# A two-layer decoder with a routed MoE on one core: scatter order, place of the overflow branch, token split and gather order changed

## The chip, the cores and the metric

The kernel runs on one core of one Trainium2 chip. The metric is the device time of one execution in microseconds (us). Engines are named as in the profile: PE is TensorE, DVE is VectorE, ACT is ScalarE, POOL is GpSimd, SP is the queue that issues the weight transfers.

## What is computed

Two layers over 256 tokens of width 1024, in float32. Each layer has a token mixer (a convolution and a pooling branch with gates) and a mixture of experts; the change lies in the second. The reference, cut to that:

```python
h2 = modulate(rms_norm(x, ffn_norm_g[l]), sh2, sc2)
x = x + g2[:, None, :] * hierarchical_moe(h2, ...)
# hierarchical_moe(t): 4 groups of 8 experts
group_probs = softmax(t @ w_rg + b_rg)
p_group, g_idx = top_k(group_probs, 1)
exp_logits = (t @ w_re + b_re).reshape(n_tok, 4, 8)
in_group = take_along_axis(exp_logits, g_idx[:, :, None], axis=1)[:, 0]
p_exp, e_idx = top_k(softmax(in_group), 2)
weights = p_group * p_exp / sum(p_exp)
out = sum over experts e of weight(t, e) * (silu(t @ w_g[e]) * (t @ w_u[e])) @ w_d[e]
```

Each token goes to two of 32 experts; an expert has a hidden width of 256, so its three matrices are 1 MB each.

## The kernel before, in words

**Weights.** All 298 MB of traffic are nearly the weights. SP issues them in a fixed order (`plan`, `issue`) into a ring of 14 slots of 1 MB and some spare tiles; a slot is filled again when PE has done with it.

**Routing** (`route`). The normalised token is split into two reduced-precision parts whose sum is the float32 value, `xhl[0]` (`xn_hi`) and `xhl[1]` (`xn_lo`): ACT writes the scaled and transposed-in-free-order copy `scr` (L765), casts it (L763), and POOL subtracts (L770). DVE finds the group and the two experts (`topk_a`, `topk_b`), PE counts how many tokens each expert has (`count`, L807), DVE turns that into a position for each of 512 token copies and builds the one-hot matrices `G2` (`place`). PE gathers the copies by `G2` (`gather`, L849: two chunks of 256 slots, eight column tiles each, high and low part), ACT and DVE apply the modulation while they copy the result to `XTp` (L855, L858). `softmax` (ACT, with two table loads) stands between the two chunks. The order in `route` is written out by hand for PE, DVE, ACT and POOL; `fill` puts pieces of PE work on later conditioning vectors (`ada_gen`, L316) into the gaps.

**Experts** (`experts`). An expert gets a window of 64 slots of the 512, wherever its tokens begin (`window`, ACT copies with a start read from a register, L1044). A block `b` is a pair of experts, 16 blocks a layer, counted from 0. PE's order within a block is by hand: 32 gate/up matmuls (L1106), of `scatter(b-1)` the parts 0 and 1 (two matmuls each, L1061 and L1062, that add the block's rows back to their tokens), two transposes (L1121), parts 2 and 3, 16 records of down matmuls (L1081). ACT and DVE are ordered by the framework's scheduler: silu (ACT L1115), times the up half and the weight (`sl`, DVE L1116), the copy of the transposed result (`aT`, DVE L1123), four adds to the residual `xs` (DVE L1069), the scatter matrix of the next block (`GT`, L1052 and L1053), and for each half of down `y` (gain, DVE L1087), its cast (ACT L1088) and the rest (`yhl`, DVE L1092). `yhl` feeds the next scatter.

**Overflow branch** (`overflow`, L980 and L981). If any expert had more than 64 tokens, PE, ACT, DVE and POOL would enter a branch that computes what the windows lost. The flag comes from `windows`. With these inputs the branch's body never runs; each of the four engines loads the flag and jumps over the body. It stands ahead of block 0, among its first gate/up matmuls.

## Time and profile before

| | |
|---|---|
| median of 3 runs | 858.16 us (857.32 to 858.34) |
| the profiled execution | 858.35 us, its span 856.6 us |
| PE busy | 775.5 us (91%) |
| DVE, ACT, POOL busy | 503.3, 279.7, 214.2 us |
| read from HBM | 296.29 MB, 347 GB/s over the span |
| the 912 gate/up matmuls of L1106 | 228.1 us busy, 10.1 us idle before them, of which 9.1 us behind PE's sequencer at L981 |

Busy shares are means over stages with different limits: the mixers, the routing, and the 32 blocks. A block's limit is read from the chain of waits, which follows each piece of work back to what released it. "issue" and an engine's name with a q (PEq) are time in its instruction queue. [...]

### The profile page before, as it was taken

How to read it: one execution, taken by the hardware profiler on the slowest of the kernel's cores; microseconds unless marked ns; L12 is line 12 of the kernel's file. 1: busy time of each engine (PE TensorE's matmuls, PEld its weight loads, DVE VectorE, ACT ScalarE, POOL GpSimd, SP SyncE). 2: the span in 40 equal slices, each digit the busy share in tenths (PEclk: the TensorE clock that was granted, in tenths of full speed). 3: DMA queues.
4: the chain of work that ended last, by engine and by line, in shares of the span. 5: the costliest groups of instructions: out<-in, count | busy, mean ns of one | idle time of the engine just before them, and what ended most of it. 6: DMA issues, size and time to landing. Idle time of an engine off the chain costs nothing. (4 is left out here: it accounts for less than half of the span.)

```text
span 856.6 us, 12068 instructions
## 1 busy us (share of the span) xinstructions
PE 775.5 (91%) x4382; PEld 444.5 (52%) x4382; DVE 503.3 (59%) x1007; ACT 279.7 (33%) x496; POOL 214.2 (25%) x151
## 2 busy tenths in 40 slices
PE   4599999989799999999979999999679999999995
PEld 1389986755233333333339998686533333333332
DVE  2359984976245545454566998497734454535454
ACT  2254544454222122212135444545422212222212
POOL 1168972540000000000034799162100000000001
PEclk9699999999899999999988999999889999999998
DMA  9999958979999999999999965797679999999981
GB/s 350 371 355 390 390 172 335 353 250 404 404 406 409 408 409 366 354 409 410 404 380 382 397 226 186 283 385 248 241 249 372 383 410 409 409 409 409 409 347 49
DMA packets 100083, 298.28 MB, mean 348 GB/s; under 512 B 13941, under 2 KB 23461, under 8 KB 100010
## 3 DMA queue, kind: packets, MB, share of 16 engines
q1 hardware_dynamic: 99448, 296.30, 90.9%
q10 hardware_dynamic: 434, 1.06, 0.3%
q8 instruction: 38, 0.62, 0.3%
q14 instruction: 35, 0.29, 0.1%
q0 software_dynamic: 128, 0.02, 0.0%
HBM read 296.29 MB, written 1.05 MB: 347 GB/s over the span
## 5 line engine op out<-in xcount | busy, mean ns | idle before, releaser
L1106 PE MATMUL pb<-wt,XTW 128*64 128x512 f32 x912 | 228.1, 601 | 10.1 <-PEq L981 9.1
L427 POOL TENSOR_TENSOR wlo<-wt,whi 128x1024 fp32r<-128x1024 f32 x60 | 147.0, 2463 | 90.4 <-ACT whi L425 66.6
L1069 DVE TENSOR_TENSOR xs<-xs,pd 128x512 f32<-128x512 f32 x124 | 82.1, 684 | 134.8 <-PE pd L1062 133.6
L1106 PEld LDWEIGHTS pb<-wt,XTW 128*64 128x64 f32 x912 | 72.9, 139 | 132.2 <-issue 126.5
L486 DVE SCALAR_TENSOR_TENSOR pd<-vpad,cols,pd 128x256 f32<-128x256 f32 x232 | 106.9, 488 | 5.7
L425 ACT CAST whi<-wt 128x1024 fp32r<-128x1024 f32 x80 | 83.0, 1050 | 73.8 <-PE pb L365 40.8
L1088 ACT CAST yhl<-y 128x512 fp32r<-128x512 f32 x64 | 39.6, 620 | 195.1 <-DVE y L1087 195.1
L1081 PE MATMUL pd<-wt,aT 128*64 128x512 f32 x320 | 94.9, 598 | 0.9 <-DVE aT L1123 0.5
L1044 ACT COPY XTW<-XTp 128x256 f32 x128 | 48.3, 406 | 131.8 <-PE pb L1106 120.3
L1092 DVE TENSOR_TENSOR yhl<-y,yhl 128x512 fp32r<-128x512 f32 x64 | 44.3, 693 | 46.1 <-ACT yhl L1088 46.0
L364 PE MATMUL pa<-hhl,whi 128*128 128x256 f32 x224 | 66.5, 297 | 5.2 <-ACT hhl L399 5.2
L316 PE MATMUL pd<-wt,cb 128*32 128x512 f32 x384 | 54.3, 655 | 14.6 <-DMA wt<-in_w_ada_dram 14.5
L1081 PE MATMUL pd<-wx,aT 128*64 128x512 f32 x192 | 65.7, 598 | 0.5 <-DVE aT L1123 0.5
L365 PE MATMUL pa<-hhl,whi 128*128 128x256 f32 x224 | 65.8, 294 | 0.3
L366 PE MATMUL pa<-hhl,wlo 128*128 128x256 f32 x224 | 64.7, 289 | 0.7 <-POOL wlo L427 0.7
L364 PE MATMUL pb<-hhl,whi 128*128 128x256 f32 x224 | 63.6, 284 | 0.0
L365 PE MATMUL pb<-hhl,whi 128*128 128x256 f32 x224 | 62.7, 280 | 0.0
L366 PE MATMUL pb<-hhl,wlo 128*128 128x256 f32 x224 | 62.6, 279 | 0.0
L1061 PE MATMUL pd<-yhl,GT 128*128 128x512 f32 x124 | 54.9, 443 | 0.6 <-ACT yhl L1088 0.6
L1081 PEld LDWEIGHTS pd<-wt,aT 128*64 128x64 f32 x320 | 27.0, 136 | 52.8 <-issue 37.2
L1168 POOL TENSOR_TENSOR xn<-xs,fz 128x512 f32<-128x512 f32 x2 | 2.6, 1284 | 189.9 <-ACT xn L353 189.9
L1087 DVE TENSOR_TENSOR y<-pd,gb 128x512 f32<-128x512 f32 x64 | 44.0, 688 | 9.9 <-PE pd L1081 9.7
(260 smaller groups left out, 1249.7 us busy)
## 6 DMA issues: line engine op xcount, KB each, us to landing
wt<-in_w_expert_gate_dram SPq DMA_DIRECT2D x114, 512.0 KB, 7.1
wt<-in_w_expert_up_dram SPq DMA_DIRECT2D x114, 512.0 KB, 11.7
wt<-in_w_ada_dram SPq DMA_DIRECT2D x48, 1024.0 KB, 11.7
wt<-in_w_expert_down_dram SPq DMA_DIRECT2D x36, 1024.0 KB, 12.4
wt<-in_w_in_dram SPq DMA_DIRECT2D x28, 1024.0 KB, 13.9
wx<-in_w_expert_down_dram SPq DMA_DIRECT2D x24, 1024.0 KB, 12.7
wt<-in_w_out_dram SPq DMA_DIRECT2D x8, 1024.0 KB, 4.9
wx<-in_w_expert_gate_dram SPq DMA_DIRECT2D x14, 512.0 KB
```

The source lines that it names most:

```text
L316: nc.tensor.matmul(ps[j:j + 32, :], cb[:, 2 * i + a, :], halves(w[:, a, :], h), start=i == 0, stop=i == 3)
L364: nc.tensor.matmul(o, ah, bh, start=start, stop=False, skip_group_check=True)
L365: nc.tensor.matmul(o, ah, bl, start=False, stop=False, skip_group_check=True)
L366: nc.tensor.matmul(o, al, bh, start=False, stop=stop, skip_group_check=True)
L425: nc.scalar.copy(hi, wv)
L427: eng.tensor_tensor(lo, wv, hi.bitcast(F32), op=OP.subtract)
L486: nc.vector.scalar_tensor_tensor(acc[:, j, :] if t == CONV_K - 1 else a, src, w, a, op0=OP.mult, op1=OP.add)
L1044: nc.scalar.copy(XTW[b % 2][:, 4 * h:4 * h + 4, CAP * j:CAP * j + CAP], r["XTp"][h][:, :, bass.ds(v, CAP)])
L1061: nc.tensor.matmul(o, GTs[b][:, tt, :], ys[b][0][:, hs], start=True, stop=False)
L1069: nc.vector.tensor_tensor(xs[:, tt, hs], xs[:, tt, hs], outs.pop(part), op=OP.add)
L1081: nc.tensor.matmul(o[64 * j:64 * j + 64, :], aTs[b][:, h, 64 * j:64 * j + 64], wv[j][:, h, :], start=h == 0, stop=h == 1)
L1106: nc.tensor.matmul(p[64 * j:64 * j + 64], XT[:, k, 64 * j:64 * j + 64], w[j][:, :, kk, :], start=k == 0, stop=k == KC - 1)
```

## The change

- The scatter: the eight matmuls of `scatter(b-1)` all stand between gate/up and the transposes. Parts 0 and 1 use the PSUM pool `pa`, parts 2 and 3 `pd`.
- The overflow branch: from ahead of block 0 to ahead of block 12 (`LATE`), where the scatter and the adds of block 11 come first. Its body (never run here) works on gathered slots, in 4 times 32 turns instead of 2 times 32.
- The token split: `xn_hi` is three ACT operations and one DVE operation of 128x512 that read `xs` in strides and write the high part at once; `xn_lo` is four DVE operations of 128x512 (scale and subtract in one) instead of four on POOL. `scr` no longer holds the scaled token.
- `topk_b(0)` stands later, `xn_lo` of the second half of the tokens after `topk_b(1)` and after `place`.
- The gather goes by contraction halves (`h`), each over both chunks, so that the first half of `XTp` is complete after the first half of the gather; window copies follow that order.
- `softmax` stands after the first window copies, in `experts`.
- The bias row of the `g2` vector (`m == 5` in `ada_gen`) is added on DVE instead of POOL; `pk` keeps both chunks' positions.

The diff, with the branch's body cut:

```diff
@@ -43,6 +43,7 @@
          1: ((0, 0), (0, 1), 0, 1, 4, 2, 5, 3, 6, 7, (1, 0), (1, 1))}
 DIV_DVE = {0, 1, 2, 3}
 FILL = (12, 24)
+LATE = 12
 TAPS1, TAPS2 = 7, 6
 ON_DVE = {2, 4, 6, 8, 30, 32, 34, 35, 36, 38}
 
@@ -319,14 +320,20 @@
             done(("ada", l, m, i))
         part = two.tile([P, 512], F32, name="part", bufs=3)
         nc.scalar.copy(part, ps)
-        if row:
+
+        def bias(eng):
             pv = part.rearrange("p (m k) -> p m k", k=4)
             for h in range(2):
                 r = slice(64 * h, 64 * h + 1)
-                nc.gpsimd.tensor_tensor(pv[r], pv[r], halves(s["brow"][r], h), op=OP.add)
+                eng.tensor_tensor(pv[r], pv[r], halves(s["brow"][r], h), op=OP.add)
+
+        if m == 2:
+            bias(nc.gpsimd)
 
         def fin():
             if row:
+                if m == 5:
+                    bias(nc.vector)
                 s["g1" if m == 2 else "g2"] = g = work.tile([P, D], F32, name="gb")
                 for h in range(2):
                     p = pd([P, 512])
@@ -728,7 +735,7 @@
         ov = rt("ov", [P, TT, NE])
         px = rt("px", [P, TT, NE])
         po = rt("po", [P, TT, 2, NE])
-        pk = rt("pk", [P, TT, 2])
+        pk = rt("pk", [P, NCHUNK, TT, 2])
         code = rt("code", [P, 2, TT, 2])
         so = rt("so", [P, NE])
         si = rt("si", [P, NE], I32)
@@ -758,16 +765,22 @@
             nc.scalar.copy(xT[:, :4, ts], tps[tt][0])
             nc.vector.tensor_copy(xT[:, 4:, ts], tps[tt][1])
 
-        def xn_hi(tt, a):
-            if a:
-                nc.scalar.copy(xhl[0][:, tt, :], scr[:, tt, :])
+        def split(tt, h):
+            hs = slice(4 * h, 4 * h + 4)
+            x = xs[:, tt, :].rearrange("p (m k) -> p k m", k=KC)[:, hs]
+            hi, lo = (t[:, tt, :].rearrange("p (k m) -> p k m", k=KC)[:, hs] for t in xhl)
+            return x, hi, lo
+
+        def xn_hi(tt, h):
+            x, hi, _ = split(tt, h)
+            if tt and h:
+                nc.vector.tensor_scalar(hi, x, rss[tt], None, op0=OP.mult)
             else:
-                nc.scalar.activation(scr[:, tt, :].rearrange("p (k m) -> p k m", k=KC),
-                                     xs[:, tt, :].rearrange("p (m k) -> p k m", k=KC), AF.Identity, scale=rss[tt])
+                nc.scalar.activation(hi, x, AF.Identity, scale=rss[tt])
 
         def xn_lo(tt, h):
-            hs = slice(h * 512, (h + 1) * 512)
-            nc.gpsimd.tensor_tensor(xhl[1][:, tt, hs], scr[:, tt, hs], xhl[0][:, tt, hs].bitcast(F32), op=OP.subtract)
+            x, hi, lo = split(tt, h)
+            nc.vector.scalar_tensor_tensor(lo, x, rss[tt], hi.bitcast(F32), op0=OP.mult, op1=OP.subtract)
 
         def router(tt):
             p = rps[tt] = pa([P, RC])
@@ -811,12 +824,12 @@
             nc.vector.tensor_reduce(out=dst, in_=po, axis=AX.X, op=OP.add)
 
         def place():
-            pick(pk, r["rp"][:, :TT, :])
+            pick(pk[:, 0], r["rp"][:, :TT, :])
             for ch in range(NCHUNK):
                 if ch:
-                    nc.vector.tensor_scalar(pk, pk, float(-SPC), None, op0=OP.add)
+                    nc.vector.tensor_scalar(pk[:, 1], pk[:, 0], float(-SPC), None, op0=OP.add)
                 for tt in range(TT):
-                    onehot(G2[:, ch], tt, pk[:, tt, :])
+                    onehot(G2[:, ch], tt, pk[:, ch, tt, :])
 
         def windows():
             nc.vector.tensor_scalar(so, r["rp"][:, 2, :], float(LAST), None, op0=OP.min)
@@ -833,15 +846,16 @@
             nc.vector.scalar_tensor_tensor(px, ov, 4096.0, r["rp"][:, :TT, :], op0=OP.mult, op1=OP.add)
             nc.vector.tensor_tensor(px, px, so[:, None, :].to_broadcast([P, TT, NE]), op=OP.subtract)
             for i, t in enumerate((io64, ioq.rearrange("p a b -> p (a b)"))):
-                cd = pen if i else lm
+                cd = pen
                 nc.vector.tensor_tensor(cd, px, t[:, None, :].to_broadcast([P, TT, NE]), op=OP.add)
                 pick(code[:, i], cd)
 
         XTp = [work.tile([P, KC // 2, NCHUNK * SPC], F32, name="XTp", tag=f"wl{h}") for h in range(2)]
 
-        def gather(ch):
-            for kp in range(KC // 2):
-                p = ((pa, pa, pd, pd), (pb, pd, pa, pa))[ch][kp]([P, 2, SPC])
+        def gather(h):
+            for z in range(4):
+                kp, ch = 2 * h + z % 2, z // 2
+                p = ((pa, pa, pd, pb), (pd, pd, pa, pa))[h][z]([P, 2, SPC])
                 for kk in range(2):
                     k = 2 * kp + kk
                     for tt in range(TT):
@@ -850,7 +864,7 @@
                                              start=kk + tt + q == 0, stop=tt + q == 2, skip_group_check=True)
                 for kk in range(2):
                     k = 2 * kp + kk
-                    dst = XTp[k // 4][:, k % 4, ch * SPC:(ch + 1) * SPC]
+                    dst = XTp[h][:, k % 4, ch * SPC:(ch + 1) * SPC]
                     if kp % 2:
                         nc.scalar.activation(dst, p[:, kk, :], AF.Identity, bias=s["B2"][:, k:k + 1],
                                              scale=s["A2"][:, k:k + 1])
@@ -858,7 +872,7 @@
                         nc.vector.tensor_scalar(dst, p[:, kk, :], s["A2"][:, k:k + 1], s["B2"][:, k:k + 1],
                                                 op0=OP.mult, op1=OP.add)
 
-        r = dict(XTp=XTp, rss=rss, lg=lg, lm=lm, gm=gm, em=em, O=O, ov=ov, po=po, code=code, si=si, rt=rt, fill=fill)
+        r = dict(XTp=XTp, rss=rss, lg=lg, lm=lm, gm=gm, em=em, O=O, ov=ov, pk=pk, po=po, code=code, si=si, rt=rt, fill=fill)
         out_mm(2, 0)
         out_mm(3, 0)
         out_add(0)
@@ -869,6 +883,7 @@
         rss.append(rms_scale(0, sss[0]))
         evac(0)
         xn_hi(0, 0)
+        xn_hi(0, 1)
         out_mm(3, 1, [0])
         out_add(1, [0])
         router(0)
@@ -881,8 +896,6 @@
         for z in (0, 64):
             nc.gpsimd.dma_start(out=s["brow"][z:z + 1, :], in_=b_ada[l:l + 1, 5 * D:6 * D])
         out_add(1, [1])
-        topk_b(0)
-        xn_hi(0, 1)
         xn_lo(0, 0)
         square(1, 1, scr[:, 1, :], sss[1])
         rss.append(rms_scale(1, sss[1]))
@@ -892,19 +905,19 @@
         evac(1)
         xn_hi(1, 0)
         xn_hi(1, 1)
-        xn_lo(1, 0)
-        xn_lo(1, 1)
+        topk_b(0)
         fill(3)
         router(1)
         topk_a(1)
         topk_b(1)
+        xn_lo(1, 0)
         fill(FILL[0])
         count()
         place()
         fill(FILL[1])
+        xn_lo(1, 1)
         windows()
         gather(0)
-        softmax(l, r)
         gather(1)
         state["routed"] = l
         issue()
@@ -980,52 +993,58 @@
         flag = nc.values_load(r["fl"][0:1, 0:1], engines=eng, min_val=0, max_val=1)
         with tc.If(flag > 0):
             xo = work.tile([P, 2, D], F32, name="xo", tag="xn")
...
+            for c in range(2 * SEQ // P):
...
                 for e in range(NE):
...
     def experts(l, r, moe):
@@ -1034,15 +1053,18 @@
         GTs, ys = {}, {}
         XTW = r["XTW"] = [work.tile([P, KC, 2 * CAP], F32, name="XTW", tag=t) for t in ("t1", "ra")]
 
-        def window(b):
+        regs = {}
+
+        def window(b, hs=range(2)):
             if b >= nb:
                 return
-            for j in range(2):
-                e = 2 * b + j
-                v = nc.values_load(r["si"][0:1, e:e + 1], engines=[E.Activation], min_val=0, max_val=LAST)
-                for h in range(2):
+            for h in hs:
+                for j in range(2):
+                    e = 2 * b + j
+                    if h == hs[0]:
+                        regs[e] = nc.values_load(r["si"][0:1, e:e + 1], engines=[E.Activation], min_val=0, max_val=LAST)
                     nc.scalar.copy(XTW[b % 2][:, 4 * h:4 * h + 4, CAP * j:CAP * j + CAP],
-                                   r["XTp"][h][:, :, bass.ds(v, CAP)])
+                                   r["XTp"][h][:, :, bass.ds(regs[e], CAP)])
 
         def prep(b):
             if b >= nb:
@@ -1057,7 +1079,7 @@
                 return
             h, tt = divmod(part, 2)
             hs = slice(h * 512, (h + 1) * 512)
-            o = outs[part] = (pa if b == nb - 2 and part > 1 else pd)([P, 512])
+            o = outs[part] = (pa if part < 2 else pd)([P, 512])
             nc.tensor.matmul(o, GTs[b][:, tt, :], ys[b][0][:, hs], start=True, stop=False)
             nc.tensor.matmul(o, GTs[b][:, tt, :], ys[b][1][:, hs], start=False, stop=True)
 
@@ -1096,6 +1118,11 @@
         def blocks():
           with tc.manual_schedule(engines={E.PE}):
             for b in range(nb):
+                if b == LATE:
+                    for part in range(4):
+                        scatter(b - 1, part)
+                        add(b - 1, part)
+                    overflow(l, r, moe)
                 p = pb([P, 2, DE])
                 XT = XTW[b % 2]
                 for h in range(2):
@@ -1114,19 +1141,17 @@
                 sl = moe.tile([P, DE], F32, name="sl", bufs=1)
                 nc.scalar.activation(sl, p[:, 0, :], AF.Silu)
                 nc.vector.scalar_tensor_tensor(sl, sl, r["ws"][:, b:b + 1], p[:, 1, :], op0=OP.mult, op1=OP.mult)
-                scatter(b - 1, 0)
-                scatter(b - 1, 1)
+                if b != LATE:
+                    for part in range(4):
+                        scatter(b - 1, part)
                 q = pt([P, 2, P])
                 for h in range(2):
                     nc.tensor.transpose(q[:, h, :], sl[:, h * P:(h + 1) * P], ident)
                 aTs[b] = moe.tile([P, 2, P], F32, name="aT", bufs=1)
                 nc.vector.tensor_copy(aTs[b], q)
-                add(b - 1, 0)
-                add(b - 1, 1)
-                scatter(b - 1, 2)
-                scatter(b - 1, 3)
-                add(b - 1, 2)
-                add(b - 1, 3)
+                if b != LATE:
+                    for part in range(4):
+                        add(b - 1, part)
                 prep(b + 1)
                 yhl = work.tile([P, 2, D], F32R, name="yhl", tag="xn")
                 ys[b] = (yhl[:, 0, :], yhl[:, 1, :])
@@ -1174,10 +1199,10 @@
           return xn, rss
 
         window(0)
+        softmax(l, r)
         weights(l, r)
         r["fill"](100)
         flush()
-        overflow(l, r, moe)
         return blocks
```

How the order moves at three places. PE in an ordinary block, from gate/up to down, before (`pb`, `pd`, `pt` and `pa` are PSUM pools, `wt` a weight tile, `GT` the scatter matrix):

```order
L1106 MATMUL pb<-wt,XTW 64x512 x16
L1061 MATMUL pd<-yhl,GT 128x512
L1062 MATMUL pd<-yhl,GT 128x512
L1061 MATMUL pd<-yhl,GT 128x512
L1062 MATMUL pd<-yhl,GT 128x512
L1121 MATMUL pt<-idc,sl 128x128 x2
L1061 MATMUL pd<-yhl,GT 128x512
L1062 MATMUL pd<-yhl,GT 128x512
L1061 MATMUL pd<-yhl,GT 128x512
L1062 MATMUL pd<-yhl,GT 128x512
L1081 MATMUL pd<-wt,aT 64x512 x8
```

and now:

```order
L1133 MATMUL pb<-wt,XTW 64x512 x16
L1083 MATMUL pa<-yhl,GT 128x512
L1084 MATMUL pa<-yhl,GT 128x512
L1083 MATMUL pa<-yhl,GT 128x512
L1084 MATMUL pa<-yhl,GT 128x512
L1083 MATMUL pd<-yhl,GT 128x512
L1084 MATMUL pd<-yhl,GT 128x512
L1083 MATMUL pd<-yhl,GT 128x512
L1084 MATMUL pd<-yhl,GT 128x512
L1149 MATMUL pt<-idc,sl 128x128 x2
L1103 MATMUL pd<-wx,aT 64x512 x8
```

The two transposes moved behind the last four scatter matmuls. DVE in the same stretch, now (before it reads the same, with all four adds from `pd`):

```order
L1091 TENSOR_TENSOR xs<-xs,pa 128x512
L1143 SCALAR_TENSOR_TENSOR sl<-sl,rtile,pb 128x256
L1091 TENSOR_TENSOR xs<-xs,pa 128x512
L1151 COPY aT<-pt 128x256
L1091 TENSOR_TENSOR xs<-xs,pd 128x512 x2
```

The first add still stands ahead of `sl`. DVE at the branch's new place, from the down of block 11 (`GT` is the scatter matrix of block 12):

```order
L1109 TENSOR_TENSOR y<-pd,gb 128x512
L1114 TENSOR_TENSOR yhl<-y,yhl 128x512
L1109 TENSOR_TENSOR y<-pd,gb 128x512
L1091 TENSOR_TENSOR xs<-xs,pa 128x512 x2
L1114 TENSOR_TENSOR yhl<-y,yhl 128x512
L1091 TENSOR_TENSOR xs<-xs,pd 128x512 x2
L1074 TENSOR_SCALAR GT<-ur,iob 128x256
L993 TENSOR_LOAD rtile
L994 COMPARE_AND_BRANCH
```

Two adds now stand ahead of the last `yhl`, which the last scatter matmuls need; on PE those come right ahead of the flag's load and the branch.

## Rows read from the trace of the kernel before

**Rows 1.** Chain of waits in order of time, layer 1, blocks 0 and 1: start, us, what.

```profile
639.19 6.87 PE pb L1106 x32
646.06 0.43 PE pd L1061
...
646.76 0.69 DVE xs L1069
...
649.26 3.58 PE pd L1081 x16
```

**Rows 2.** Chain of waits, the last block of layer 1.

```profile
838.69 0.43 PE pd L1061
...
839.82 0.32 PE pt L1121 x2
840.13 0.23 PE pa L1061
...
841.07 1.89 PE pd L1081 x8
```

**Rows 3.** Timeline of PE, layer 1, gather's end to block 0: start, us, what [idle before].

```profile
615.08 1.88 PE L333 MATMUL pd<-part,Q 128*128 128x512 f32 x4
...
625.06 7.60 PE L1106 MATMUL pb<-wt,XTW 128*64 128x512 f32 x22 [4.30 <-PEq L981]
632.59 1.07 PE L966 MATMUL pd<-rtile,rq 128*128 128x16 f32 x8
...
634.61 0.41 PE L1121 MATMUL pt<-idc,sl 128*128 128x128 f32 x2
635.54 3.65 PE L1081 MATMUL pd<-wt,aT 128*64 128x512 f32 x16 [0.52 <-DVE aT L1123]
```

**Rows 4.** Lines L980, L981 (ns min/median/max, first and last start); timeline of PE's weight loads.

```profile
L980 PEldq TENSOR_LOAD <-rtile x2: 310/400/490, 211.7 to 613.4; - x2
L981 PEldq COMPARE_BRANCH  x2: 6102/6118/6133, 212.6 to 618.8; - x2
...
618.77 0.25 PEld L1106 LDWEIGHTS pb<-wt,XTW 128*64 128x64 f32 x4 [0.61 <-ACT XTW L1044]
```

**Rows 5.** Windows: us, busy of PE, PEld, DVE, ACT, POOL, PEclk, DMA share, GB/s.

```profile
235.00:320.00 85.00, 80.75 (x366) 30.30 (x364) 41.17 (x73) 18.83 (x45) 0.31 (x1) 1.00 1.03 408
625.00:632.00 7.00, 6.94 (x21) 2.38 (x22) 1.60 (x8) 2.16 (x6) 0.00 (x0) 0.67 0.55 166
```

**Rows 6.** Timeline of DVE, down of block 1 in layer 1.

```profile
653.22 0.68 DVE L1087 TENSOR_TENSOR y<-pd,gb 128x512 f32<-128x512 f32 x1
654.59 0.69 DVE L1092 TENSOR_TENSOR yhl<-y,yhl 128x512 fp32r<-128x512 f32 x1 [0.69 <-ACT yhl L1088]
```

**Rows 7.** Timeline of DVE and POOL, routing of layer 1 (first and last of four).

```profile
594.04 0.25 DVE L795 SCALAR_TENSOR_TENSOR rtile<-io,rtile 128x32 bf16<-128x32 f32 x1
...
598.46 1.32 DVE L791 TENSOR_TENSOR rtile<-io,rtile 128x64 f32<-128x64 f32 x1
...
602.21 1.30 DVE L795 SCALAR_TENSOR_TENSOR rtile<-io,rtile 128x32 bf16<-128x32 f32 x1
...
598.44 2.48 POOL L770 TENSOR_TENSOR xhl<-scr,xhl 128x512 fp32r<-128x512 f32 x2 [2.13 <-ACT xhl L763]
```

**Rows 8.** Groups by line and form: busy us, mean ns of one.

```profile
L765 ACT ACTIVATE scr<-xs,rs 128x1024 f32<-128x1024 f32 x4 | 9.0, 2244 | 4.0 <-POOL rs L359 4.0
L763 ACT CAST xhl<-scr 128x1024 fp32r<-128x1024 f32 x4 | 4.2, 1047 | 1.7 <-PE pt L365 1.7
```

**Rows 9.** Timeline of ACT, gather of layer 1.

```profile
612.54 1.28 ACT L930 ACT_TABLE_LOAD   x1
```

**Rows 10.** Timelines of SP and PE, block 15 of layer 0; the page's DMA issues.

```profile
415.99 0.33 SPq L114 DMA_DIRECT2D wt<-in_w_expert_up_dram  x1
...
423.46 7.04 PE L1106 MATMUL pb<-wt,XTW 128*64 128x512 f32 x32
...
wt<-in_w_expert_up_dram SPq DMA_DIRECT2D x114, 512.0 KB, 11.7
```

## The prediction

> **What bounds the kernel now.** I read the busy shares first (PE 91%), then the chain of waits backwards from the end, then PE's timeline where that chain leaves PE. In an expert layer the chain is PE's own. A block is 32 gate/up matmuls (6.87 us), 3.20 us from there to the first down matmul, and 3.58 us of down [rows 1]: a period of 13.65. In the 3.20 PE stands for about 0.7 behind a DVE add, because DVE takes `xs` ahead of `sl` [rows 1]. Block 15 runs its eight scatter matmuls nearly without a gap and gets from gate/up to down in 841.07 - 838.69 = 2.38 [rows 2].

> Ahead of block 0 PE stands for 4.30 us behind its own sequencer, and the 22 gate/up matmuls behind the branch take 632.59 - 625.06 = 7.53 [rows 3] where a block's rate gives 22/32 x 6.87 = 4.72. [...] DMA is the second limit: in layer 0's blocks it moves 408 GB/s at a full share [rows 5], while a block consumes six 1-MB matrices, 6.29 MB, in 13.65 us, or 460 GB/s.

> **The change, part by part.**

> *Scatter order (12 blocks a layer: 1 to 11 and 13).* All eight scatter matmuls now stand between gate/up and the transposes. They cost 839.82 - 838.69 = 1.13 for the first four and 841.07 - 840.13 = 0.94 for the rest [rows 2], 2.07 in sum. DVE still takes one `xs` add ahead of `sl`, but it now runs under the scatters: the add starts about 0.7 behind gate/up, `sl` is done near 1.8, before the 2.07. Then transposes and `aT` copy, from 634.61 to down at 635.54, 0.93 [rows 3], no longer covered. 6.87 + 2.07 + 0.93 + 3.58 = 13.45: **-0.2 a block**. Bounds: 0 (another add slips ahead) and -0.7 (the add's whole wait goes). Blocks 14 and 15 lose: their order was better, 2.38 [rows 2] becomes 3.0, **+0.6 each**.

> *Routing.* Four small DVE operations, from 598.46 to the end of the last at 603.51, take 5.05 us beside GpSimd's split; the last takes 1.30 there and 0.25 when GpSimd is idle [rows 7]. Without GpSimd the four take 1 us: -4. In exchange DVE gets five 128x512 operations of strided `xs`. The trace has no such DVE operation; ScalarE's strided 128x1024 takes 2.24 where the contiguous cast takes 1.05 [rows 8]. Half of the former is 1.1, and I take 1.2 each, 6 us; bounds 0.7 (an `xs` add, [rows 1]) to 1.3. Most of them lie where DVE waits for PE; I put 1.5 on the path, so the gather starts 2.5 earlier (bounds -4 and +1, all six on the path), and ends 3.0 earlier, since the first evacuations are spread over both engines.

> [...]

> *Behind the gather.* From the last gather matmuls to down of block 0 it takes 635.54 - 615.08 = 20.46 [rows 3]. The softmax's two table loads, the first 1.28 long [rows 9], stand ahead of the last evacuations and the window copies; now they stand behind the copies. What is left for PE is the bias product 1.88, gate/up 6.87, and 635.54 - 632.59 = 2.95 for spread, transposes and `aT` [rows 3], 11.7; with 1.8 allowed for the other transposes and the last copies, 13.5. That is -7.0; with the gather's end **-10.0 in layer 1** (9 to 12).

> *Layer 0* has the same pieces, but DMA caps it. The last `up` tile of block 15 is issued at 415.99 and lands by the median 11.7 later, 427.7; that block's gate/up starts at 423.46 and needs it halfway, near 427 [rows 10]. So at block 15 next to nothing is spare. A block needs 6.29 MB / 408 GB/s = 15.4 us of DMA for 13.65 of PE, so four blocks earlier there are 4 x 1.77 = 7.1 us, plus up to 3 by which tiles may land under the median. I take **-10 at block 11**, blocks' gain included. In layer 1 the same count leaves 12, which holds -10.0 and eleven blocks' 2.2.

> *The branch at block 12.* It now stands behind scatter(11), which waits for `yhl` of block 11. Counted from the first down matmul (D): DVE ends `y` at 653.90, D + 4.64 [rows 6]; two `xs` adds of 0.69 [rows 1] are now queued between it and the last `yhl` (0.69, [rows 6]), so that ends at D + 6.7. Then the branch, 6.1 [rows 4], and gate/up starts at D + 12.9 instead of D + 3.58: +9.3. The matmuls behind it meet the lower clock again: 7.53 - 4.72 = 2.8 before [rows 3], 2.3 taken, as a part of that waited for window copies which now come earlier. Behind gate/up no scatter is left, 1.9 instead of 3.20: -1.3. Sum **+10.3 a layer**. Bounds: the flag's load, 0.4 [rows 4], not overlapped, and 2.8 (+11.2); branch hidden under the wait, full clock (+2). DVE's own branch (its `GT` half is behind it) ends long before `sl` of block 12 is due.

> *The g2 bias on DVE* is two 1x512 operations while PE works on the gather: nothing, or 1.4 by two adds if they fell on the path.

> *Sum.* Layer 0: -10 + 10.3 - 0.2 + 1.2 = +1.3. Layer 1: -10.0 - 2.2 + 10.3 - 0.2 + 1.2 = -0.9. Together +0.4. The profiled execution took 858.35 (the median of the runs is 858.16, 0.2 lower): **858.7, no change that can be told**. A measurement here tells 0.2%, 1.7 us.

> **Rivals.**

> 1. *Faster: the branch runs under the wait for block 11's `yhl`.* Then 6.1 a layer goes. Against it: in layer 1 the flag was loaded at 613.4, yet the branch began at 618.8, when PE's weight load at 618.77 had been released by ACT's copy [rows 4]; the branch seems to follow the last met wait. Layer 0 can use only some 2 to 3 of the gain (DMA), layer 1 all: 858.7 - 3 - 6.1 = 849.6, about 850. [...] Chance 0.2.

> 2. *Slower: the split on DVE takes back the routing's gain.* All five strided operations, 6.0, on the path to the gather, against 4 that GpSimd's absence gives back: the gather ends 2 later instead of 3 earlier, 5 a layer. In layer 0 the cap had already taken 1.5 of that. 858.7 + 5 + 3.5 = 867 at worst; with half of it hidden, 863. It decides once more than 1.5 + 2.5 = 4 of the 6 us are waited for. For it: a price of 1.2 on the engine that sets the count's start; against: DVE idles between the router's steps. Chance 0.14.

> 3. *Slower: the branch costs more at its new place.* The body that it jumps over has twice the matmuls (128 turns against 64). If the 6.1 goes with that length, it is 12.2: +6.1 a layer, 871. Both branches before jump over the same body, so no row tells. Chance 0.06.

> 4. *The blocks do not get shorter*, because DVE still adds before `sl`: 2.4 us of layer 1 are lost, layer 0 being held by DMA: 861. Chance 0.1.

> **How the numbers follow.** The forecast has 0.5, its own range 855.5 (the routing gives 12 in layer 1 and the clock costs nothing in one layer) to 861 (9, and the branch +11.2 in each): of it faster has 0.17, same 0.24, slower 0.09. Rival 1 adds 0.2 to faster, rivals 2 and 3 add 0.2 to slower; rival 4 puts 0.03 in same and 0.07 in slower. Faster 0.37, same 0.27, slower 0.36. The range leaves out rival 3 and the far ends of 1 and 2: 850.5 to 863.5.

> **What would show it.** Right: PE's branch at block 12 lasts 6.1, gate/up of block 12 starts 12 to 14 behind down(11), the clock is low behind it; down of block 0 in layer 1 comes 10 earlier; a block's period is 13.45; gate/up ahead of block 12 in layer 0 waits for DMA little or not at all. Wrong: a branch that begins before scatter(11)'s last wait; DVE's split on the path to the count; a period still at 13.65; PE waiting for weights for several us in layer 0, with nothing gained by routing.

## The result, and the profile after

The changed kernel takes 868.57 us (median of 4 runs, 866.49 to 871.69) against 858.16 for the kernel before (median of 3; a fourth run of it took 1570.39 and is left out); the ratio is 1.0122, 95% interval 1.0104 to 1.0141. It is slower by about 10 us, where 858.7 and "no change" were forecast. The profiled execution took 867.65, its span is 865.9.

The table gives the start of the first down matmul of a block, read from PE's timeline, and in brackets the period to the block before (for block 0 of layer 1, to block 15 of layer 0). It answers to [rows 1 to 3].

| block | before | after | after minus before |
|---|---|---|---|
| layer 0, 0 | 229.38 | 220.83 | -8.6 |
| layer 0, 10 | 365.92 (13.65) | 354.08 (13.32) | -11.8 |
| layer 0, 11 | 379.57 (13.65) | 369.41 (15.33) | -10.2 |
| layer 0, 12 | 393.23 (13.65) | **399.57 (30.17)** | +6.3 |
| layer 0, 15 | 432.82 (12.85) | 439.53 (13.32) | +6.7 |
| layer 1, 0 | 635.54 (202.72) | 633.62 (194.09) | -1.9 |
| layer 1, 11 | 787.79 (13.65) | 782.30 (13.32) | -5.5 |
| layer 1, 12 | 801.45 (13.65) | **808.16 (25.86)** | +6.7 |
| layer 1, 13 | 815.10 (13.65) | 823.18 (15.02) | +8.1 |
| layer 1, 15 | 841.00 (12.82) | 849.80 (13.31) | +8.8 |

Up to block 11 the times go nearly as forecast: the stretch ahead of block 0 is shorter by 8.6 in each layer, an ordinary block by 0.33. (The forecast puts the 8.6 down to the routing. The run with the branch alone moved, below, shows that nearly all of it comes from the branch no longer standing there.) At block 12 both gains are lost again and more: 16.5 in layer 0, 12.2 in layer 1, and 1.4 more at block 13 there. The branch itself is as long as before [rows 4], though its body has doubled (line L994 of the changed kernel; ns min/median/max, first and last start):

```profile
L994 PEldq COMPARE_BRANCH  x2: 6040/6046/6052, 377.0 to 789.6; - x2
L994 DVEq COMPARE_BRANCH  x2: 63/68/72, 377.7 to 790.4; - x2
...
L994 PEldq EVENT_SEMAPHORE  x2: 51/51/51, 383.1 to 795.8; - x2
L994 DVEq EVENT_SEMAPHORE  x2: 21/21/21, 383.3 to 796.0; - x2
```

The timeline of PE around it, layer 0 first, then layer 1 (start, us, what, idle before and its releaser):

```profile
376.05 0.50 PE L1084 MATMUL pd<-yhl,GT 128*128 128x512 f32 x1 [0.72 <-DVE yhl L1114]
...
376.62 0.40 PE L1084 MATMUL pd<-yhl,GT 128*128 128x512 f32 x1
383.36 1.08 PE L1133 MATMUL pb<-wx,XTW 128*64 128x512 f32 x1 [6.34 <-DMA wx<-in_w_expert_down_dram]
388.90 1.01 PE L1133 MATMUL pb<-wx,XTW 128*64 128x512 f32 x1 [4.46 <-issue]
```

```profile
788.93 0.50 PE L1084 MATMUL pd<-yhl,GT 128*128 128x512 f32 x1 [0.73 <-DVE yhl L1114]
...
789.51 0.40 PE L1084 MATMUL pd<-yhl,GT 128*128 128x512 f32 x1
796.01 1.09 PE L1133 MATMUL pb<-wx,XTW 128*64 128x512 f32 x1 [6.10 <-PEq L994]
```

In both layers PE waits for block 11's last `yhl`, 6.6 us behind the down's start (376.05 - 369.41, 788.93 - 782.30), as forecast (6.7). Then comes the branch. The 6.34 that the profile puts down to a DMA in layer 0 is this same wait: PE's sequencer was in the branch from 377.0 to 383.1. But in layer 0 PE stands idle a second time, for 4.46 (called a hole below), behind the first gate/up matmul, with the releaser "issue": PE waited for nothing that the profile shows. And the clock falls (windows: us, busy of PE, PEld, DVE, ACT, POOL, PEclk, which is the granted share of PE's full clock, DMA share, GB/s):

```profile
377.00:383.00 6.00, 0.02 (x1) 0.00 (x0) 1.14 (x3) 0.00 (x0) 0.00 (x0) 0.62 1.03 405
383.00:389.00 6.00, 1.18 (x2) 0.29 (x3) 0.48 (x1) 0.00 (x0) 0.00 (x0) 0.50 1.02 404
796.00:802.00 6.00, 5.99 (x16) 2.65 (x18) 0.48 (x1) 0.00 (x0) 0.00 (x0) 0.52 1.03 406
808.00:812.00 4.00, 3.84 (x10) 1.16 (x12) 0.59 (x2) 0.00 (x0) 0.00 (x0) 0.57 1.03 410
```

In layer 1 the first 16 gate/up matmuls of block 12 run almost wholly at the lower of the two clock levels (0.52; in the traces of both kernels every record of the granted clock is 0.50 or 1.00), and the clock is low once more in down of block 12 (0.57 from 808 to 812), which makes block 13 late (15.02).

The routing, for [rows 3, 7, 8] (timeline of PE in layer 1; groups by line and form, busy us, mean ns):

```profile
608.05 0.18 PE L820 MATMUL pb<-rtile,onesb 128*128 128x32 bf16 x1 [0.60 <-DVE rtile L808]
...
610.61 3.86 PE L863 MATMUL pa<-G,xhl 128*128 128x256 f32 x16 [2.16 <-DVE G L931]
...
618.09 2.05 PE L863 MATMUL pa<-G,xhl 128*128 128x256 f32 x16
621.54 7.54 PE L1133 MATMUL pb<-wt,XTW 128*64 128x512 f32 x32 [1.40 <-ACT XTW L1066]
```

```profile
L783 DVE SCALAR_TENSOR_TENSOR xhl<-xs,rs,xhl 128x512 fp32r<-128x512 f32 x8 | 9.3, 1161 | 0.0
L779 ACT ACTIVATE xhl<-xs,rs 128x512 fp32r<-128x512 f32 x6 | 7.3, 1245 | 11.0 <-PE pt L372 8.6 <-POOL rs L366 2.5
L777 DVE TENSOR_SCALAR xhl<-xs,rs 128x512 fp32r<-128x512 f32 x2 | 1.4, 682 | 0.0
```

From block 15 of layer 0 the gather now starts 610.61 - 439.53 = 171.08 behind, instead of 605.70 - 432.82 = 172.88: 1.8 earlier, and from its end (618.09 + 2.05) to down it takes 633.62 - 620.14 = 13.5, where 20.3 stood (635.54 - 615.25; 20.46 in [rows 3] is counted from the bias product).

### The profile page after: what moved, and what is told of

The parts are those of the page before. It is cut to its first block, busy times and chain, and to the rows that moved or that the text cites. A ratio compares the mean times of both kernels' runs of the same rounds, so it can differ in the third digit from the quotient of the medians.

```text
span 865.9 us, 12021 instructions
## 1 busy us (share of the span) xinstructions
PE 777.8 (90%) x4382; PEld 455.4 (53%) x4382; DVE 504.7 (58%) x1021; ACT 273.2 (32%) x494; POOL 200.2 (23%) x139
## 3 DMA queue, kind: packets, MB, share of 16 engines
q10 hardware_dynamic: 434, 1.06, 0.3%
HBM read 296.29 MB, written 1.05 MB: 343 GB/s over the span
## 5 line engine op out<-in xcount | busy, mean ns | idle before, releaser
L1133 PEld LDWEIGHTS pb<-wt,XTW 128*64 128x64 f32 x912 | 75.8, 138 | 125.8 <-issue 119.2
L1091 DVE TENSOR_TENSOR xs<-xs,pa 128x512 f32<-128x512 f32 x64 | 43.2, 683 | 126.2 <-PE pa L1084 126.2
L1133 PE MATMUL pb<-wx,XTW 128*64 128x512 f32 x112 | 52.4, 640 | 16.9 <-DMA wx<-in_w_expert_down_dram 6.3
L1109 DVE TENSOR_TENSOR y<-pd,gb 128x512 f32<-128x512 f32 x64 | 44.0, 688 | 10.3 <-PE pd L1103 8.6
## 6 DMA issues: line engine op xcount, KB each, us to landing
wt<-in_w_ada_dram SPq DMA_DIRECT2D x48, 1024.0 KB, 11.7
wt<-in_w_expert_down_dram SPq DMA_DIRECT2D x36, 1024.0 KB, 12.9
```

The source lines that it names most:

```text
L1109: nc.vector.tensor_tensor(y, downs.pop(n), s["g2"][:, n * 512:(n + 1) * 512], op=OP.mult)
L1133: nc.tensor.matmul(p[64 * j:64 * j + 64], XT[:, k, 64 * j:64 * j + 64], w[j][:, :, kk, :], start=k == 0, stop=k == KC - 1)
```

## The experiments

Theory A: what the branch costs at block 12 is (1) the wait for `yhl`, (2) the branch, (3) in layer 0 a second wait for instructions, because the code behind the branch begins a few instructions ahead of the end of a 16-KB block of PE's program (the instruction queue q8 moves packets of 16 KB: 39 of them, 0.64 MB, in the changed kernel), so that PE waits for the next block as well, and (4) the low clock behind the idle time. Theory B: the second hole is a wait for weights, as the releaser of the first suggests.

The kernel before took 859.0 to 859.8 beside the experiments and 858.2 beside the changed kernel, so totals of different experiments compare to some 1.5 us.

What stands in favour of A ahead of any run: in the changed kernel's trace q8 moves two packets of 16 KB between 376 and 392 us, and they start at 380.5 and 386.3, the second 2.6 us ahead of the matmul at 388.90.

```profile
q8 instruction: 2, 0.03, 0.9%
```

**No branch at all.** `LATE = 99`, so the call is never made; the kernel leaves out the path for overfull experts.

> The changed kernel without the overflow branch (left out: the path for experts with more than 64 tokens; every block then has the ordinary order). Theory A (the branch at block 12 costs all that the rest gains): the periods of block 12 fall from 30.2 and 25.9 us to 13.3, down of block 0 stays where it is in layer 0 (220.8); layer 0 then waits for weights from block 11 on and keeps about 3 of its 11 us, layer 1 keeps all: 841 to 846 us. Theory B (the 5.5 us of PE idle behind the branch in layer 0 are a wait for weights): the same idle time shows up in blocks 11 to 13 of layer 0 without any branch, and the total is 849 or more.

Measured: 845.94 us, ratio 0.9847 (0.9809 to 0.9885). Block 12 has 15.34 and 13.32, and layer 0 shows the DMA limit plainly: blocks 11 to 15 have periods of 16.33, 15.34, 15.48, 15.54, 15.37, near the 15.4 that 6.29 MB need at 408 GB/s. PE's groups of that stretch (366 to 434 us) name it:

```profile
L1133 PE MATMUL pb<-wt,XTW 128*64 128x512 f32 x121 | 32.6, 595 | 4.3 <-DMA wt<-in_w_expert_up_dram 4.3
```

So the changed kernel without any branch is some 14 us faster than the kernel before with its branch (the 14 hold what that branch cost ahead of block 0), and the branch takes some 23 of the changed kernel. Theory A's total holds, at the end of its range (841 to 846); block 12 of layer 0 does not fall to 13.3, as the weights hold it.

**Code behind the branch shifted.** In layer 0, ahead of the branch:

```diff
+                    if l == 0:
+                        z = pa([P, 512])
+                        for i in range(8):
+                            nc.tensor.matmul(z[:, :8], ident, ident[:, :8], start=True, stop=True)
                     overflow(l, r, moe)
```

> The changed kernel with eight tiny matmuls (16 PE instructions, 128x8, result unused) in layer 0 right ahead of the branch, so that the code behind the branch lies 16 instructions later. Theory A (the code behind the branch begins a few instructions before the end of a 16-KB block of instructions, and PE waits for the next block): the 5.5 us of idle in layer 0 go, its block-12 period falls from 30.2 to 24 or 25, the total by 4 to 6, to 862 to 864 us. Theory B (a wait for weights): the idle time stays, 867 to 869.

Measured: 862.89 us, ratio 1.0042 (1.0026 to 1.0059), 5.7 less than the changed kernel and in Theory A's range. (The eight products are 16 matmuls and 16 loads in the program, so the shift is 32 instructions.) Layer 0's block 12 falls from 30.17 to 25.36, layer 1's stays (25.83). The hole behind the first matmul is gone (timeline of PE, layer 0):

```profile
377.93 1.85 PE L1128 MATMUL pa<-idc 128*128 128x8 f32 x16
384.77 1.08 PE L1137 MATMUL pb<-wx,XTW 128*64 128x512 f32 x1 [5.00 <-PEq L994]
384.90 1.08 PE L1137 MATMUL pb<-wt,XTW 128*64 128x512 f32 x1
385.65 1.06 PE L1137 MATMUL pb<-wx,XTW 128*64 128x512 f32 x1
```

The weights and their order are the same: B falls. A block holds 256 instructions, by an estimate from the run without a branch: PE runs 8966 there (4382 matmuls, 4382 loads, 202 of its sequencer), and q8 moves 35 packets of 16 KB, 8960 at 256 each. In the changed kernel's trace PE runs a median of 250 instructions from the start of one packet to the next. The table counts the instructions of PE's program from the end of the jump to the end of their block, with one offset fitted to layer 0 of the changed kernel. No kernel with more than 50 left shows such a hole (59 is the least, in layer 1 of the kernel before with the branch alone moved). The traces agree without that count: among the 22 jumps of all these kernels, the before included, the four with a hole are those of the table, and PE gets through 5, 5, 18 and 32 instructions between the branch's end and the hole, within 4 of the count:

| kernel, layer | instructions left in the block | hole behind the branch |
|---|---|---|
| changed, 0 | 5 | 4.46 after 1 matmul |
| changed, 1 | 126 | none |
| branch ahead of block 0, 1 | 2 | 4.31 after 1 matmul |
| branch behind down(11), 0 | 17 | 2.34 after 7 matmuls |
| twelve products, 1 | 28 | 0.91 after 14 matmuls |
| shifted, 0 | 228 | none |

**Work queued across the branch.** Twelve, then six products of 128x512 with unused result between scatter(11) and the branch, in both layers:

```diff
+                    z = pa([P, 512])
+                    for i in range(12):
+                        nc.tensor.matmul(z, ident, s["g2"][:, :512], start=True, stop=True)
                     overflow(l, r, moe)
```

> The changed kernel with twelve matmuls of 128x512 (result unused, some 0.47 us each, 5.6 in sum) behind scatter(11) and ahead of the branch in both layers, so that PE has work queued while the branch is processed. If the branch starts while they are queued and the granted clock follows PE's idle time: the clock behind the branch stays at the full level, gate/up of block 12 takes 6.9 instead of 9.8, total 860 to 865 us (the 24 instructions also move the code behind the branch, which may take away the 5.5 us of layer 0). If the branch is processed only when they are done: 5.6 more a layer, 873 to 879.

Measured: 868.37 us, ratio 1.0100 (1.0065 to 1.0136): neither total. One product is two records of 0.44, so the twelve take 10.5 us and not 5.6. They show two things. The branch runs while matmuls are queued: it starts at 792.6, when 16 of the 24 records are still to run, and the next gate/up waits 0.30 only (timeline of PE, layer 1). And the clock stays full (1.00 from 780 to 808): block 13 has 13.32 again. So the run was repeated with half of them.

```profile
789.25 10.46 PE L1127 MATMUL pa<-gb,idc 128*128 128x512 f32 x24
800.01 0.61 PE L1136 MATMUL pb<-wx,XTW 128*64 128x512 f32 x1 [0.30 <-PEq L994]
```

> The changed kernel with six instead of twelve of the unused 128x512 products behind scatter(11) (12 matmul records of 0.44 us each in the run before, 5.2 us in sum), about as long as the branch. Theory A: the branch (6.05) runs while they are queued, so gate/up of block 12 starts when it did without them (13.7 to 14.3 us behind down(11)), but at the full clock: block 12 has a period of 23 to 24 us in layer 1 instead of 25.9 and block 13 13.3 instead of 15.0; in layer 0 the code behind the branch lies far from the end of its 16-KB block (238 instructions left), so 23 to 24 instead of 30.2. Total 856 to 860 us. If the low clock costs nothing, layer 1 stays at 25.9 and the total is 862 or more.

Measured: 857.00 us, ratio 0.9981 (0.9971 to 0.9991), 11 us less than the changed kernel, by matmuls that compute nothing. Block 12 takes 23.35 and 23.11, block 13 13.3 in both. Gate/up starts behind the branch at the same distance from down(11), 13.8 (timeline of PE, then windows of this kernel and of the changed one):

```profile
783.23 5.31 PE L1127 MATMUL pa<-gb,idc 128*128 128x512 f32 x12
789.60 0.61 PE L1136 MATMUL pb<-wx,XTW 128*64 128x512 f32 x1 [1.06 <-PEq L994]
```

```profile
789.00:796.00 7.00, 6.40 (x30) 3.98 (x32) 0.00 (x0) 0.71 (x2) 0.00 (x0) 1.00 1.02 403
```

```profile
789.00:796.00 7.00, 0.90 (x3) 0.44 (x4) 1.55 (x3) 0.00 (x0) 0.00 (x0) 0.68 1.03 405
796.00:804.00 8.00, 7.99 (x24) 3.53 (x26) 0.48 (x1) 0.71 (x2) 0.00 (x0) 0.64 1.03 406
```

The low clock (0.64 to 0.68 instead of 1.00) thus cost 25.86 - 23.11 = 2.75 at block 12 and 1.7 at block 13 of layer 1. In layer 0 the products also move the code behind the branch away from the end of its block (238 instructions left, by the count), so the 11 us are the sum of both effects.

**The branch back ahead of block 0.** `LATE = 99`, and the call behind `flush()` in `experts`, as before the change.

> The changed kernel with the branch ahead of block 0, as before the change, all other parts kept. Theory A: block 12 has the ordinary period in both layers; the branch costs up to 4.3 of waiting and 2.8 of low clock at block 0 as before, less where PE has gate/up queued ahead of it; 845 to 852 us. Theory B: layer 0 still stands for some 5 us at block 12: 855 or more.

Measured: 862.29 us, ratio 1.0030 (1.0009 to 1.0051): the total missed by 10. Block 12 is ordinary in both layers (13.32), so B fails here too, but block 0 is late by 8.6 in layer 0 and 12.5 in layer 1 against no branch. ACT, DVE and PE reach the branch later in the new order than in the old one; PE has all 32 gate/up matmuls of block 0 behind it and waits for DVE's `rq`. In layer 0 that comes 5.8 us behind the start of DVE's own branch (217.1 and 222.9). In layer 1 DVE's branch is done at 628.1, but `rq` comes at 630.8, released by the end of PE's branch, which takes 6.8 there. In layer 1 the code behind the branch also lies at the end of a block (2 instructions left, in the table; timeline of PE):

```profile
631.21 0.37 PE L979 MATMUL pd<-rtile,rq 128*128 128x16 f32 x1 [5.76 <-DVE rq L975]
635.89 1.47 PE L979 MATMUL pd<-rtile,rq 128*128 128x16 f32 x7 [4.31 <-issue]
```

**The branch alone moved, in the kernel before.** The same lines as in the change (four parts of scatter and add, then `overflow`, at block 12), all else as before.

> The kernel before with the branch alone moved to block 12 (its body as before). Theory A: block 12 has a period of 25 to 27 in both layers (last yhl, 6.05 of branch, low clock), block 13 up to 1.7 more, against some 7 saved ahead of block 0 in each layer; no second instruction wait, since the code behind the branch begins far from the end of a 16-KB block here: 866 to 872 us. If the loss needed the other parts (DVE adds in a different place, the longer body), 860 or less.

Measured: 869.72 us, ratio 1.0126 (1.0109 to 1.0143). Block 12 has 25.73 and 24.70 in the profiled execution, which took 864.75, the shortest of the five. The loss comes with the branch's place; it needs neither the new routing nor the longer body.

The run also shows what gave the 8.6 ahead of block 0. It has the old routing, gather and softmax, and yet block 0 of layer 0 comes at 221.96, 7.4 ahead of the kernel before, and block 0 of layer 1 comes 194.46 behind block 15 of layer 0, where the kernel before has 202.72 and the changed kernel 194.09. From the gather's end to down it takes 13.5, as in the changed kernel (timeline of PE, layer 1):

```profile
615.88 2.05 PE L850 MATMUL pa<-G,xhl 128*128 128x256 f32 x16
620.65 7.88 PE L1112 MATMUL pb<-wt,XTW 128*64 128x512 f32 x32 [1.00 <-ACT XTW L1045]
631.40 1.94 PE L1082 MATMUL pd<-wt,aT 128*64 128x512 f32 x8 [0.56 <-ACT ur L975]
```

So the branch's leaving is worth 7.4 and 8.3. The new routing's own share is 1.1 to 2.7 in layer 0 (219.2 to 220.9 in the seven kernels that have it with no branch and no added work ahead of block 0) and nothing clear in layer 1 (194.1 to 195.4 in the same seven). No run has the new routing alone.

**The scatter order alone, in the kernel before.**

> The kernel before with the scatter order and its PSUM pools alone changed. From the changed kernel's rows: blocks 1 to 13 have a period of 13.33 instead of 13.65 in both layers, blocks 14 and 15 13.3 instead of 13.1 and 12.8; 3.5 us less in layer 1, at most 2.7 to 3.5 in layer 0, where weights arrive little ahead at block 15: 851 to 853 us. If the period came from the other parts of the change, it stays 13.65: 858.

Measured: 856.15 us, ratio 0.9964 (0.9948 to 0.9980). The period is 13.32 or 13.33 up to block 13 in both layers (block 10 of layer 1 apart, which has other work, before and after); in layer 0 it is given back at blocks 14 and 15 (14.49 and 15.31, waits for weights), so layer 1's 3.5 us are what remains. The total was 3 above the range given; the kernel before took 859.6 in the same runs, so the gain is 3.5, and layer 0's share was overrated.

**The branch behind gate/up of block 12.** The call with scatter(11) and its adds moved from ahead of the block's gate/up to behind it.

> The changed kernel with the branch behind gate/up of block 12 and scatter(11), the four adds of block 11 ahead of it on DVE and sl of block 12 behind it. If only PE's branch counts, it runs under gate/up and scatter for 2 to 4 us and costs 3 to 4: period of block 12 some 17 us, total 849 to 853. If DVE's own branch (about 5.5 us from its start to its next instruction) is on the path once sl stands behind it: down of block 12 some 8 us late, period 20 to 22, total 853 to 858.

Measured: 862.27 us, ratio 1.0036 (1.0023 to 1.0050), period of block 12 20.88 in layer 1. The second reading holds for the period: PE's branch was done at 796.7, 2 us behind the last scatter, but DVE's lasted to 800.7, and `sl` stood behind it (timeline of PE):

```profile
801.73 0.69 PE L1149 MATMUL pt<-idc,sl 128*128 128x128 f32 x2 [7.09 <-DVE sl L1143]
```

The total is above both ranges: block 13 is late (15.10 and 15.56; in layer 1 the 16 down matmuls of block 12 take 5.44 instead of 3.65, as at a low clock), and in layer 0 `aT` came another 3.9 late (period 26.62): two instructions behind its branch DVE stood for 4.17 with the releaser "issue". That this is a second wait for instructions, as on PE, was not tested.

**The branch right behind down(11).** Scatter(11) stays in its ordinary place; the branch's body takes its scratch from the idle window buffer:

```diff
                 if b == LATE:
-                    for part in range(4):
-                        scatter(b - 1, part)
-                        add(b - 1, part)
                     overflow(l, r, moe)
...
-                if b != LATE:
-                    for part in range(4):
-                        scatter(b - 1, part)
+                for part in range(4):
+                    scatter(b - 1, part)
...
-            xo = work.tile([P, 2, D], F32, name="xo", tag="xn")
-            wsp, y = xo[:, 0], xo[:, 1]
+            wsp = r["XTW"][(LATE + 1) % 2].rearrange("p a c -> p (a c)")
```

> The changed kernel with the branch right behind down of block 11 and scatter(11) in its ordinary place behind gate/up of block 12 (the branch's body takes its scratch from the idle window buffer, so that it need not wait for block 11's scatter). Theory A: the branch starts about 1 us behind the start of down(11), while its matmuls are queued, and ends near 7; gate/up of block 12 starts 3.5 late instead of 10 to 15, DVE's branch lies in its pause. Layer 0 waits for weights there anyway. By the place of the code in its 16-KB block (19 instructions are left) a second wait of some 4 us comes in layer 0, none in layer 1. 848 to 854 us, less than both kernels; the rival (the branch waits until PE is idle) gives 855 to 858.

Measured: 853.78 us, ratio 0.9936 (0.9916 to 0.9956), faster than both kernels. Layer 1 (timeline of PE): the branch starts at 778.0, 1.3 behind the first down matmul, and gate/up 7.6 behind it instead of 13.7:

```profile
779.78 0.59 PE L1103 MATMUL pd<-wx,aT 128*64 128x512 f32 x1
784.33 1.08 PE L1130 MATMUL pb<-wx,XTW 128*64 128x512 f32 x1 [3.96 <-PEq L994]
```

The low clock still takes 1.6 there (period 19.09 = 13.32 + 4.1 + 1.6), by an estimate; the first six gate/up matmuls last 1.06 to 1.09 each, where 0.59 is ordinary.

> The same with 24 tiny matmuls (result unused) in layer 0 ahead of the expert count, where PE waits for DVE, so that the code behind the branch moves by 48 instructions and 227 are left in its 16-KB block in layer 0, 84 in layer 1. Theory A: no second instruction wait in layer 0; as weights limit layer 0 behind block 11, the total changes little: 0 to 4 less than the kernel without the shift, 847 to 852 us. If the wait behind the branch in layer 0 stays, instruction blocks are not its cause.

The edit: twelve of the tiny products ahead of `count()` in layer 0. Measured: 853.05 us, ratio 0.9929 (0.9906 to 0.9951), 0.7 less than without the shift as forecast (0 to 4), though the total is 1 above the range given. Block 12 of layer 0 takes 19.51 instead of 22.07, without a hole: the second test that instructions, not weights, are the cause. The tiny products also bring block 0 4.2 later. Blocks 14 and 15 then wait for weights (14.33 and 15.36), and block 15 comes at 432.72 instead of 432.82, so the DMA hides both. It does not hide all that the branch costs in layer 0: without a branch block 15 comes at 430.64.

## Why the prediction was wrong, step by step

- **Branch at block 12: the step that failed.** It was forecast at +10.3 a layer with bounds of +2 and +11.2, and measured 16.5 and 12.2 + 1.4 against the old period, 30.1 in place of 20.6. That is nearly all of the miss, 868.6 - 858.7 = 9.9. The mechanism was right in its first two steps, the wait for `yhl` (6.6 measured, 6.7 forecast) and the branch (6.05, 6.1). Missed were the second instruction wait in layer 0, 4.8 by the shifted kernel; the clock, put at 2.3 from the old branch's stretch ([rows 3, 5]) and worth 2.75 to 2.9 plus the fall at block 13, 1.4 to 1.7; and small steps in the queue, 0.8 to 1.0: gate/up starts 13.7 and 13.95 behind down(11) instead of 12.9. The upper bound was built from one row's low clock and put the wait for the next block of instructions behind the jump at nothing.
- **Scatter order:** -0.2 forecast, -0.33 measured; right in kind, and the reason was right (the add under the scatters).
- **Blocks 14 and 15:** +1.2 in layer 1 forecast, 0.24 + 0.49 = 0.7 measured.
- **Routing:** -10.0 forecast in layer 1, -8.6 measured, but not for the reason given. The 20.46 behind the gather held the old branch (4.30 of waiting and 2.8 of low clock, by the prediction's own lines), and the 13.5 that was to be left held none. So the -7.0 is the branch's leaving. The softmax's place, named as the cause, gives nothing that can be seen: 13.5 with the softmax in its old place and the branch gone. The four small DVE operations did fall to 0.9 (607.11 to 608.00), as forecast. The gather started 1.8 earlier instead of 2.5, but 1.9 earlier with the old routing too. That the number came near was luck in part.
- **DMA cap in layer 0:** -10 at block 11 forecast, -10.2 measured; without a branch it is the DMA's 15.4 a block.
- **The tail behind block 15** was not forecast to change and is 0.5 longer.
- **Rival 1** (branch under the wait) did not occur here: scatter(11)'s waits hold the sequencer (the branch starts 0.9 and 0.7 behind the release of the last one, 376.05 to 377.00 and 788.93 to 789.64). Its condition was found by experiment: the branch does run under queued matmuls whose waits are met, 16 of them in the twelve-product run, where the branch starts at 792.6 and the products end at 799.7.
- **Rival 3** (cost by the body's length) named a total near the measured one for a reason that the rows refute on PE: 6.05 with the double body. On ACT the jump did get longer, from 1.2 and 1.7 us over the old body (kernel before) to 5.2 over the new one, but nothing waited for it.
- **Rival 2** holds in part: the gather of layer 1 ends 1.8 earlier than before (180.6 behind block 15 of layer 0, before 182.4), but with the old routing and the branch moved it ends at 181.0, so the new routing as a whole gains nothing clear there. Its total of 863 to 867 is not how the loss came about.
- **Rival 4** is refuted by the period of 13.32.
- **The range:** by its own terms the forecast's inner range is 854.4 to 861.5 (858.7 - 2 - 2.3, 858.7 + 1 + 2 x 0.9), not 855.5 to 861. The result lies outside either.

The jump's price is 6.05 us on PE here, with a packet of q8 that starts 3.5 us behind the branch's start (377.0 and 380.5). That PE also waits for the next block when the target lies near the end of its own is shown by the runs above: 0.91 to 4.46 us with 28 to 2 instructions left.

## What to carry to other kernels

A branch that is never entered still costs every engine its jump, in the changed kernel 6.05 us on PE, 5.6 on DVE, 5.2 on ACT and 5.3 on POOL; it was cheaper where each engine had work queued without open waits or paused anyway (853.78 us, right behind down(11)), and dear behind an instruction that waited (868.57). When code moves, look at where the instruction behind a jump lies in its 16-KB block (a hole of 0.91 to 4.46 us here), and at the clock behind the idle time (2.75 us at block 12 of layer 1). A stall can be mostly hidden by DMA in one layer and paid in the other: with the branch right behind down(11), block 12 of layer 0 takes 6.7 us more than without a branch (22.07, 15.34) and block 15 comes 2.2 later (432.82, 430.64), while in layer 1 of the changed kernel the 12.2 at block 12 and the 1.4 at block 13 are still there at block 15 (-5.5 at block 11, +8.8 at block 15). And when a change has several parts, run each part alone before a gain is put down to one of them: here the branch's leaving passed for a gain of the routing.
